# Opening the pool of layer 1's modulation weights ahead of layer 0's down-phase pools, and issuing its first loads there

## The chip, the cores and the metric

The kernel runs on one core of one Trainium2 chip. The metric is the device time of one execution in microseconds (us), the median of several runs. The core has five engines that each execute their own instructions in order: TensorE (PE, with weight loads listed as PEld), VectorE (DVE), ScalarE (ACT), GpSimd (POOL) and SyncE (SP). Nearly all transfers are issued by SP, in its order, as DMAs.

## The reference, cut to what matters

Two layers work on 512 latent and 256 context tokens of width 1024. Each has a mixing part and a feed-forward part, and six modulation vectors come from a product of the conditioning vectors with `ada_w`, 1024 by 6144 per layer.

```python
for l in range(DEPTH):
    mod_l = (jax.nn.silu(c) @ ada_w[l] + ada_b[l])[:, None, :]
    mod_c = (jax.nn.silu(c_ctx) @ ada_w[l] + ada_b[l])[None, None, :]
    sh1, sc1, gt1, sh2, sc2, gt2 = jnp.split(mod_l, 6, axis=-1)
    ...
    p_l = modulate(rms_norm(lat, norm_mix_pre[l]), sh1, sc1) @ w_in[l]
    ...
    mixed_l = jnp.concatenate([gla_l, ssd_l, ret_l], axis=-1) @ w_out[l]
    lat = lat + gt1 * rms_norm(mixed_l, norm_mix_post[l])
    h_l = modulate(rms_norm(lat, norm_ffn_pre[l]), sh2, sc2)
    lat = lat + gt2 * rms_norm(swiglu(h_l, ffn_w13[l], ffn_w2[l]), norm_ffn_post[l])
```

## The kernel before, in words

All tokens stay on one core, as six blocks of 128. Float32 products are made from two rounded parts, a high and a low one (`whi` and `wlo` of weights, `hidhi` and `hidlo` of the hidden activations, two `H` tiles of the normed input), in three matmuls each. A scheduler orders the instructions of each engine by a time model and the priorities of the program's order; the order that it chose is what the engines execute.

Modulation. Layer 0's vectors 0 and 1 are made at the start. The others are made in "steps" by the class `Ada`: a step takes one block of 128 by 1024 weights, `araw` (512 KB), loaded at L195, and multiplies it with the conditioning vectors in four small matmuls (L203 and L206), eight steps to a vector, into the accumulator `pa`. `pa` comes from a pool of one buffer (L93), `araw` from three (`NRAW`, L248). `ada.some(n)` puts n steps at a place of the program; inside, up to three loads are issued ahead of the first step. After eight steps `ada_finish` (L208) takes the accumulator out: for the two gate vectors it clears a tile on GpSimd, loads the bias into it in four pieces (L216), adds the sums on VectorE (L217) and stores the row in four pieces (L219); for the others ScalarE copies it (L221). Layer 0 makes its own vectors 2 to 5 and layer 1's 0 and 1 (48 steps), layer 1 its own 2 to 5 (32 steps), first the gate 2.

Pools. `adp` of a layer (opened at L595) holds a table of constants, `cst2` (843 KB), and the `araw` tiles; once the mixing part is over, `cst2` and two `araw` buffers hold parts of the feed-forward's input, `b11h` and `b11l` (L1197, L1198), for the up phase. It is closed at L1419, and the pools of the down phase are opened where it lay (`D0` at L1420). Layer 1's `adp` is opened at the head of layer 1, in the place that the down phase's pools have left; a new tile waits for the tiles that it overlaps.

Down phase of layer 0. Two passes of 512 columns read the hidden activations back from DRAM (`hr`, two loads of 768 KB at a time) and multiply them (L1407). The second pass ends in the back part, `ffn_back`, block by block: post-norm, addition to the residual rows `x` (L337), a store to `xsd` (L338), and layer 1's first norm: ScalarE's `xn`, eight transposes (L306), modulation (L312 and L314), and the split into `H` (L317 and L318). The rows `x` are loaded from `xsd` (L322) into two buffers. Layer 1 begins with the projection `gv` (L644; L498 into `mm`), 24 matmuls for each of the six blocks, and with `small` (72 matmuls), whose results ScalarE copies out at L681.

Of the kernel before, what the change touches and what calls it, by code (L numbers as in the profile page):

```python
# [77 lines left out]
CST, COFF, MSK = _constants()  # L78
NC0 = COFF["ident"][1]
# [3 lines left out]
def tile_backbone(ctx: ExitStack, tc: tile.TileContext, a: dict, out: bass.AP, dbg=None):  # L83
    nc = tc.nc
    V, S, G, PE, DMA = nc.vector, nc.scalar, nc.gpsimd, nc.tensor, nc.sync
# [15 lines left out]
    def pt(pool, tag, shape, dt=F32, bufs=None):  # L101
        kw = {} if bufs is None else {"bufs": bufs}
        return pool.tile(shape, dt, tag=tag, name=tag, **kw)

    def pool(name, bufs=1, side="left"):
        return tc.tile_pool(name=name, bufs=bufs, side=side, reuse_waits="tile")
# [4 lines left out]
    cst = [pt(pp, "cst", [128, NC0])]  # L111
# [6 lines left out]
    def C(k, shape=None, **ax):  # L118
        o, n = COFF[k]
        v = cst[0][:, o:o + n] if o < NC0 else cst[1][:, o - NC0:o - NC0 + n]  # L120
        return v.rearrange(shape, **ax) if shape else v
# [6 lines left out]
    def hpair():  # L128
        t = [pt(hp, "H", [128, 8, T], F32R) for _ in range(2)]
        return t, [h.bitcast(F32) for h in t]  # L130
# [60 lines left out]
    def ada_load(ap, l, kind, part, nparts, k0, bufs):  # L191
        w = 1024 // nparts
        c0 = 1024 * kind + w * part
        raw = pt(ap, "araw", [128, nparts, w], bufs=bufs)
        DMA.dma_start(raw, kblk(a["ada_w"][l, 128 * k0:128 * (k0 + nparts), c0:c0 + w]))  # L195
        return raw

    def ada_step(ps, raw, kb, g_w):
        first = None
        for g in range(4):  # L200
            args = ps[32 * g:32 * g + 32, :g_w], sil[:, kb, :], raw[:, g_w * g:g_w * g + g_w]
            if first is None:
                first = PE.matmul(*args, start=kb == 0, stop=kb == 7)  # L203
            else:
                with tc.high_priority(offset=2000), tc.issue_after(first.ins):
                    PE.matmul(*args, start=kb == 0, stop=kb == 7)  # L206
# [41 lines left out]
    NRAW = 3  # L248

    class Ada:  # L250
        def __init__(self, ap, tasks):
            self.ap = ap
            self.todo = [(l, kind, kb) for l, kind in tasks for kb in range(8)]
            self.raws = []

        def some(self, n):
            for _ in range(min(n, len(self.todo))):
                while len(self.raws) < min(NRAW, len(self.todo)):
                    l, kind, kb = self.todo[len(self.raws)]
                    self.raws.append(ada_load(self.ap, l, kind, 0, 1, kb, NRAW))  # L260
                l, kind, kb = self.todo.pop(0)
                if kb == 0:
                    self.ps = psa.tile([128, 512], F32, tag="pa", name="pa")
                ada_step(self.ps, self.raws.pop(0)[:, 0], kb, 256)
                if kb == 7:
                    ada_finish(self.ap, l, kind, 0, 1, self.ps, NRAW)

    def kblk(src):
        return src.rearrange("(k p) n -> p k n", p=128)
# [50 lines left out]
    def x_tile(np_, xin, bufs=2):  # L320
        x = pt(np_, "x", [128, D], bufs=bufs)
        DMA.dma_start(x, xin)  # L322
        return x
# [17 lines left out]
    def load_gw(gp, np_, l, w, rs_):  # L341
        gw = pt(gp, "gw", [128, 2, D], bufs=1)
        wpt = pt(np_, "xn", [128, D])
        src = a["norm_mix_post"] if w == 0 else a["norm_ffn_post"]
        DMA.dma_start(wpt, src[l:l + 1, :].to_broadcast([128, D]))
        for r in rs_:
            DMA.dma_start(gw[:, r], gts[l, w, r:r + 1, :].to_broadcast([128, D]))
            G.tensor_tensor(gw[:, r], gw[:, r], wpt, ALU.mult)
        return gw
# [233 lines left out]
    G.tensor_copy(msk, mskf)  # L583
    st_.close()

    for l in range(NL):
        last = l == NL - 1
        u = U[l]
# [2 lines left out]
        segs_out = [LAT] if last else [LAT, CTX]  # L591
        tbs_all = [4, 5, 0, 1, 2, 3]
        tbs_out = [0, 1, 2, 3] if last else tbs_all
        ax = ctx.enter_context(ExitStack())
        adp = ax.enter_context(pool(f"adp{l}", 2))  # L595
        cst[1:] = [pt(adp, "cst2", [128, CST.shape[1] - NC0], bufs=1)]
        S.dma_start(cst[1], a["cst"][:, NC0:])
        ones = C("ones")
        tri = C("tri", "p (a f) -> p a f", a=2)
        gam = C("gam", "p (h f) -> p h f", h=4)  # L600
# [46 lines left out]
        with ExitStack() as sx:  # L647
# [134 lines left out]
            with pool(f"Sb{l}") as Sb, tc.high_priority(offset=300):  # L782
# [23 lines left out]
                def ssd_out(tb, Sf, Sbw):  # L806
# [47 lines left out]
                                            bc(eG[:, tb, 8 * d:8 * d + 8], 64), ALU.mult)  # L854
                            (V if d else G).tensor_tensor(y, y, y1, ALU.add)
                    DMA.dma_start(yds[l][tsl, :], y)

                ada = Ada(adp, [(l, kind) for kind in range(2, 6)] + ([] if last else [(l + 1, 0), (l + 1, 1)]))

                sf = sb = None  # L860
                for tbs in ([4, 5], [0, 1, 2, 3]):
# [410 lines left out]
        def hid_load(hr, f, q=None):  # L1272
            return DMA.dma_start(hr, hview[:, f:f + 2])

        def hid_split(hr, hi, lo):
            for q in range(2):
                S.copy(hi[:, q], hr[:, q])  # L1277
                (G if q else V).tensor_tensor(lo[:, q], hr[:, q], hi[:, q].bitcast(F32), ALU.subtract)  # L1278
            return hi, lo
# [137 lines left out]

        fx.close()
        ax.close()  # L1419
        with pool(f"D{l}") as Dp:  # L1420
            y0 = pt(Dp, "y0", [128, npos, 512], bufs=1)

            order = [f for pi in range(2) for f in range(0 if pi else 4, NF, 2)]
            fetched = []

            def hid_fetch():
                if order:
                    hr = pt(Dp, "hr", [128, 2, tot], bufs=2)
                    ins = hid_load(hr, order[0])
                    fetched.append((order.pop(0), hr))  # L1430
                    return ins.ins

            def hid_pair(f):
                g, hr = fetched.pop(0)
                assert g == f
                pair = hid_split(hr, *(pt(Dp, t, [128, 2, tot], F32R, bufs=3) for t in ("hidhi", "hidlo")))
                hid_fetch()
                return pair

            with tc.high_priority(offset=60):  # L1440
                hid_fetch()
                fetch2 = hid_fetch()

            dx = ctx.enter_context(ExitStack())
            back = {}

            def begin_back():
                nf = dx.enter_context(pool(f"nf{l}", 2))
                gw = load_gw(Dp, nf, l, 1, [0] if last else [0, 1])
                if last:  # L1450
                    xs = [x_tile(nf, xsd[128 * tb:128 * tb + 128, :], 4) for tb in tbs_out]
                else:
                    H["t"], H["f"] = hpair()

                def ffn_back(pos, ps):
                    tb = tbs_out[pos]
                    tsl = slice(128 * tb, 128 * tb + 128)
                    dst = out[0, tsl, :] if last else xsd[tsl, :]
                    cut = last and pos == npos - 1
                    x = xs[pos] if last else x_tile(nf, xsd[tsl, :])  # L1460
                    x = post_norm(nf, [y0[:, pos], ps], x, gw[:, 0 if tb < 4 else 1], dst, cut)
                    if not last:
                        pre_norm(nf, l + 1, 0, tb, x)

                return ffn_back

            for pi, (j, poss) in enumerate(u["passes"]):
                pss = first if pi == 0 else acc_tiles(pi)
                if pi == 1:
                    back = begin_back()  # L1470
                f = 0
                for gi, gn in enumerate(GROUPS):
                    if pi or gi > 1:
                        with nullcontext() if pi or gi > 2 else tc.issue_after(fetch2):
                            un = get(u["w2"][gi, pi])
                    ks = [k0 for k0 in range(0, gn, 2) if pi or f + k0 >= 4]
                    if gi + 1 < len(GROUPS):
                        for k0 in ks:
                            hh = hid_pair(f + k0)
                            for pos, ps in zip(poss, pss):  # L1480
                                down(ps, hh, un, k0, pos, f + k0)
                    else:
                        hs = [hid_pair(f + k0) for k0 in ks]
                        prev = None
                        for pos, ps in zip(poss, pss):
                            for k0, hh in zip(ks, hs):
                                down(ps, hh, un, k0, pos, f + k0)
                            if j == 0:
                                (S.copy if pos % 2 else V.tensor_copy)(y0[:, pos], ps)
                                continue  # L1490
                            if prev is not None:
                                back(*prev)
                            prev = pos, ps
                        if prev is not None:
                            back(*prev)
                    f += gn
            dx.close()
# [20 lines left out]
```

## Time and profile before

| | |
|---|---|
| median of 3 runs | 1870.13 us (1869.07 to 1879.29) |
| the profiled execution, its own time | 1874.65 us |
| its span, first to last instruction | 1872.9 us |
| mean granted TensorE clock, share of full | 0.962 |
| PE busy | 1740.0 us (93%) |
| DVE busy | 1170.5 us (62%) |
| ACT busy | 793.2 us (42%) |
| POOL busy | 571.0 us (30%) |

The times in all views are counted from the span's start. A row of the view of stretches gives the stretch, its length, then the busy time of PE, PEld, DVE, ACT and POOL with the number of instructions in brackets, and last the granted clock as a share of full speed, the busy share of the 16 DMA engines and GB/s. A row of the timeline gives start, duration, engine, line, operation, output<-input, shape and the number of merged instructions; in brackets stands the idle time before it and what ended it. "SPq" is the issue of a DMA, not its transfer. Matmul durations overlap, so two successive starts tell the pace. A grouped row gives a line's instructions with their number, busy time, mean duration in ns, and then the engine's idle time before them with its causes. A row of the DMA view gives the transfers issued, their number and the size of each.

### The profile page before, as it was taken

What the parts mean: (1) busy time and instruction counts of PE and PEld (TensorE: products, weight loads), DVE (VectorE), ACT (ScalarE), POOL (GpSimd) and SP (SyncE); (2) the same over time, 40 slices, a digit from 0 to 9 for tenths busy, and PEclk for the clock granted to TensorE, in tenths of its full rate; (3) what the DMA queues carried; (4) which work ended last, traced back from release to release, by engine and by line L of the source; (5) the groups of instructions that cost most, each with busy time, mean ns of one, the idle gap of its engine ahead of it and who ended that gap; (6) DMA issues with size and microseconds to landing.
All of it is one profiled execution on the core that took longest, in us unless ns stands there. A gap on an engine that the chain in (4) does not pass through costs nothing. (4 is left out here: it accounts for less than half of the span.)

```text
span 1872.9 us, 30314 instructions
## 1 busy us (share of the span) xinstructions
PE 1740.0 (93%) x11851; PEld 1571.3 (84%) x11851; DVE 1170.5 (62%) x1981; ACT 793.2 (42%) x1433; POOL 571.0 (30%) x569
## 2 busy tenths in 40 slices
PE   5999899998879999999999989999987979999998
PEld 3778887798868999999888767898876969999886
DVE  4586777467557755555433436678856567888455
ACT  3545343225654333333333466444424544444343
POOL 1002622114403433222422240073303126555322
PEclk9999998999989999999999989999977979999999
DMA  8435476514324433332746373355613245444753
GB/s 288 175 103 172 130 214 216 185 46 163 128 68 132 135 94 113 104 94 64 270 138 200 112 230 130 113 159 160 228 47 119 89 125 161 125 132 130 249 203 133
DMA packets 239228, 275.15 MB, mean 147 GB/s; under 512 B 14056, under 2 KB 182476, under 8 KB 239084
## 3 DMA queue, kind: packets, MB, share of 16 engines
q1 hardware_dynamic: 237872, 271.30, 45.2%
q8 instruction: 93, 1.52, 0.3%
q10 hardware_dynamic: 1212, 1.91, 0.3%
q14 instruction: 51, 0.42, 0.1%
HBM read 234.24 MB, written 38.93 MB: 146 GB/s over the span
## 5 line engine op out<-in xcount | busy, mean ns | idle before, releaser
L369 DVE TENSOR_TENSOR wlo<-raw,whi 128x1024 fp32r<-128x1024 f32 (+2 forms) x192 | 266.6, 1395 | 154.0 <-ACT whi L368 153.7
L1324 PE MATMUL px<-H,whi 128*128 128x384 f32 (+1 forms) x1408 | 307.4, 310 | 9.7 <-ACT whi L368 9.5
L368 ACT CAST whi<-raw 128x1024 fp32r<-128x1024 f32 (+2 forms) x192 | 193.9, 1018 | 221.0 <-PE px L1324 86.0
L498 PE MATMUL mm<-whi,H 128*128 128x256 f32 x1376 | 273.9, 294 | 9.7 <-ACT stg L630 4.6
L1324 PEld LDWEIGHTS px<-H,whi 128*128 128x128 f32 x1408 | 235.2, 190 | 12.2 <-ACT whi L368 11.5
L498 PEld LDWEIGHTS mm<-whi,H 128*128 128x128 f32 x1376 | 223.6, 196 | 23.8 <-issue 11.3
L1324 PE MATMUL px<-H,wlo 128*128 128x384 f32 (+1 forms) x704 | 211.1, 310 | 0.0
L498 PE MATMUL mm<-wlo,H 128*128 128x256 f32 x688 | 200.7, 292 | 0.0
L498 PE MATMUL mm<-H,whi 128*128 128x256 f32 (+2 forms) x640 | 160.8, 341 | 6.3 <-ACT xp L759 4.2
L368 ACT CAST whi<-S 128x1024 fp32r<-128x1024 f32 x88 | 73.5, 835 | 165.0 <-DVE S L419 85.0
L498 PEld LDWEIGHTS mm<-wlo,H 128*128 128x128 f32 x688 | 135.4, 197 | 3.7 <-issue 2.9
L1324 PEld LDWEIGHTS px<-H,wlo 128*128 128x128 f32 x704 | 131.3, 190 | 0.7 <-DVE wlo L369 0.6
L498 PEld LDWEIGHTS mm<-H,whi 128*128 128x128 f32 (+1 forms) x640 | 109.4, 190 | 25.5 <-ACT xp L759 6.0
L498 PE MATMUL px<-whi,H 128*128 128x256 f32 x640 | 121.2, 289 | 9.6 <-DVE H L1236 4.4
L1278 POOL TENSOR_TENSOR hidlo<-hr,hidhi 128x768 fp32r<-128x768 f32 (+1 forms) x40 | 70.8, 1771 | 178.0 <-ACT hidhi L1277 167.1
L1359 POOL TENSOR_TENSOR hf<-hf,g 128x384 f32<-128x384 f32 (+1 forms) x44 | 55.8, 1269 | 224.4 <-issue 147.0
L369 DVE TENSOR_TENSOR wlo<-S,whi 128x1024 fp32r<-128x1024 f32 x88 | 89.3, 1015 | 40.6 <-ACT whi L368 40.5
L498 PEld LDWEIGHTS px<-whi,H 128*128 128x128 f32 x640 | 101.2, 193 | 13.7 <-ACT H L1235 6.3
L498 PE MATMUL mm<-H,wlo 128*128 128x256 f32 (+3 forms) x320 | 108.5, 339 | 0.0
L1407 PE MATMUL px<-wlo,hidhi 128*128 128x512 f32 x276 | 107.5, 389 | 0.0
L1407 PE MATMUL px<-whi,hidhi 128*128 128x512 f32 x276 | 106.4, 389 | 0.0
L1407 PE MATMUL px<-whi,hidlo 128*128 128x512 f32 x276 | 105.7, 389 | 0.0
(334 smaller groups left out, 4089.4 us busy)
## 6 DMA issues: line engine op xcount, KB each, us to landing
raw<-ffn_w_dram SPq DMA_DIRECT2D x100, 512.0 KB
araw<-ada_w_dram SPq DMA_DIRECT2D x96, 512.0 KB
raw<-w_in_dram SPq DMA_DIRECT2D x26, 1024.0 KB
raw<-ffn_w_dram SPq DMA_DIRECT2D x20, 1024.0 KB
hr<-hd SPq DMA_DIRECT2D x22, 768.0 KB
hr<-hd SPq DMA_DIRECT2D x22, 512.0 KB
Rt<-gd SPq DMA_DIRECT2D x40, 256.0 KB
hd<-hf SPq DMA_DIRECT2D x22, 384.0 KB
```

Of the source, the lines that this page charges most:

```text
L368: S.copy(hi, src)
L369: lo_engine.tensor_tensor(lo, src, hi.bitcast(F32), ALU.subtract)
L498: PE.matmul(ps, x(k), y(k), start=(k == 0 and p == 0), stop=(k == total - 1 and p == 2))
L1278: (G if q else V).tensor_tensor(lo[:, q], hr[:, q], hi[:, q].bitcast(F32), ALU.subtract)
L1324: PE.matmul(ps[:, :hn], w[x][:, k], r[y](k), start=first and k == 0 and p == 0, stop=k == 3 and p == 2, skip_group_check=True)
L1359: G.tensor_tensor(h1, h1, g1, ALU.mult)
L1407: PE.matmul(ps, lh[x](k), rh[y](k), start=f + k == 0 and p == 0, stop=f + k == NF - 1 and p == 2, skip_group_check=True)
```

## The change

Layer 1's `adp` is opened before the pools of layer 0's down phase, right where layer 0's is closed, and so lies in its place beside them; its table of constants is loaded there. The `Ada` of a layer is made with the pool. A new method `fetch` issues the loads that the buffers have room for, and is called for layer 1's at the second pass of layer 0's down phase. The calls of `some` stay where they were.

```diff
+        def fetch(self):
+            while len(self.raws) < min(NRAW, len(self.todo)):
+                l, kind, kb = self.todo[len(self.raws)]
+                self.raws.append(ada_load(self.ap, l, kind, 0, 1, kb, NRAW))
+
         def some(self, n):
             for _ in range(min(n, len(self.todo))):
-                while len(self.raws) < min(NRAW, len(self.todo)):
-                    l, kind, kb = self.todo[len(self.raws)]
-                    self.raws.append(ada_load(self.ap, l, kind, 0, 1, kb, NRAW))
+                self.fetch()
...
+    def open_ada(l):
+        ax = ctx.enter_context(ExitStack())
+        adp = ax.enter_context(pool(f"adp{l}", 2))
+        cst[1:] = [pt(adp, "cst2", [128, CST.shape[1] - NC0], bufs=1)]
+        S.dma_start(cst[1], a["cst"][:, NC0:])
+        return ax, adp
...
-        ax = ctx.enter_context(ExitStack())
-        adp = ax.enter_context(pool(f"adp{l}", 2))
-        cst[1:] = [pt(adp, "cst2", [128, CST.shape[1] - NC0], bufs=1)]
-        S.dma_start(cst[1], a["cst"][:, NC0:])
+        if l == 0:
+            ax, adp = open_ada(0)
+            ada = Ada(adp, [(l, kind) for kind in range(2, 6)] + [(l + 1, 0), (l + 1, 1)])
...
-                ada = Ada(adp, [(l, kind) for kind in range(2, 6)] + ([] if last else [(l + 1, 0), (l + 1, 1)]))
...
         fx.close()
         ax.close()
+        if not last:
+            ax, adp = open_ada(l + 1)
+            ada = Ada(adp, [(l + 1, kind) for kind in range(2, 6)])
         with pool(f"D{l}") as Dp:
...
                 if pi == 1:
                     back = begin_back()
+                    if not last:
+                        ada.fetch()
```

The scheduler moves more than the three loads. On SP, in the back part, the kernel before has these rows (`x_10173` and `x_10219` are the residual rows of the fifth and sixth block, `araw_12143` the weights of layer 1's first step):

```order
L338 DMA xsd_89<-x_10057 128x1024
L322 DMA x_10173<-xsd_89 128x1024
L338 DMA xsd_89<-x_10115 128x1024
L322 DMA x_10219<-xsd_89 128x1024
L640 DMA vd1_93<-stg_10317 128x256
L338 DMA xsd_89<-x_10173 128x1024
L640 DMA vd1_93<-stg_10345 128x256
L195 DMA araw_12143<-ada_w_dram 128x1024
L195 DMA araw_12145<-ada_w_dram 128x1024
L195 DMA araw_12147<-ada_w_dram 128x1024
```

The same place of the changed kernel (`x_10184` and `x_10230` are the fifth and sixth block; `araw_12172`, `12178`, `12380` and `12386` the weights of steps 7 to 10, `araw_12392` the bias row after step 8, `araw_12403` step 11):

```order
L195 DMA araw_12172<-ada_w_dram 128x1024
L195 DMA araw_12178<-ada_w_dram 128x1024
L195 DMA araw_12380<-ada_w_dram 128x1024
L341 DMA xsd_89<-x_10126 128x1024
L325 DMA x_10184<-xsd_89 128x1024
L195 DMA araw_12386<-ada_w_dram 128x1024
L216 DMA araw_12392<-ada_b_dram 2x256 x3
L325 DMA x_10230<-xsd_89 128x1024
L216 DMA araw_12392<-ada_b_dram 2x256
L341 DMA xsd_89<-x_10184 128x1024
L219 DMA gts_88<-araw_12392 2x256 x4
L195 DMA araw_12403<-ada_w_dram 128x1024
```

Before, the loads of the steps stood behind all `x` loads; now loads 4 to 6 stand ahead of these rows, 7 to 10 between them, and from load 11 on they follow the gate's stores. The first three loads stand at the end of the up phase, around its last but one `hd` store.

On TensorE, the kernel before has its first step here, after the first block of the latents is begun (`mm_10348` is the third block's projection):

```order
L498 MATMUL mm_10348<-whi_9897,H_9448 128x256
L306 MATMUL px_10195<-cst_75,xn_10193 128x128 x4
L306 MATMUL px_10207<-cst_75,xn_10193 128x128 x4
L498 MATMUL mm_10348<-whi_9901,H_9447 128x256
L498 MATMUL mm_10348<-wlo_9902,H_9447 128x256
L203 MATMUL pa_12149<-araw_12143,sil_104 32x256
L206 MATMUL pa_12149<-araw_12143,sil_104 32x256 x3
L498 MATMUL mm_10348<-whi_9901,H_9448 128x256
```

In the changed kernel this is the place of step 17, the first into the accumulator `pa_12559`, with what stands ahead of it and behind it (`xn_10250` is the sixth block; the rows for steps 13 to 15 stand between the transposes and the first row):

```order
L203 MATMUL pa_12405<-araw_12434,sil_104 32x256
L206 MATMUL pa_12405<-araw_12434,sil_104 32x256 x3
L203 MATMUL pa_12559<-araw_12538,sil_104 32x256
L206 MATMUL pa_12559<-araw_12538,sil_104 32x256 x3
L501 MATMUL mm_10354<-whi_9908,H_9452 128x256
L501 MATMUL mm_10354<-wlo_9909,H_9452 128x256
L501 MATMUL mm_10354<-whi_9908,H_9453 128x256
```

Steps 1 to 3 now stand right behind the last matmul of the down phase, and all of steps 1 to 17 stand ahead of the projections of the last four blocks (`mm_10354` is the first of them) and of `small`; before, eight steps stood in this stretch, the first of them inside the third block's projection.

## Rows read from the trace of the kernel before

**Rows 1.** Stretches: length, PE, PEld, DVE, ACT, POOL, clock, DMA, GB/s.

```profile
877.00:887.00 10.00, 10.00 (x60) 10.00 (x59) 3.50 (x7) 2.64 (x5) 1.01 (x1) 1.00 0.11 41
905.00:922.00 17.00, 17.00 (x76) 14.04 (x76) 7.62 (x5) 5.38 (x7) 9.96 (x5) 1.00 0.93 343
1070.25:1124.75 54.50, 43.35 (x327) 36.80 (x327) 22.58 (x45) 33.99 (x74) 22.54 (x28) 0.87 0.71 226
1091.00:1103.00 12.00, 6.42 (x38) 5.17 (x37) 3.74 (x8) 6.02 (x12) 4.61 (x4) 0.72 0.91 308
1125.00:1250.00 125.00, 122.29 (x805) 104.34 (x804) 85.88 (x129) 63.37 (x105) 27.25 (x33) 0.99 0.41 130
1370.00:1430.00 60.00, 42.34 (x246) 35.14 (x246) 36.36 (x92) 19.32 (x43) 6.08 (x13) 0.66 0.21 68
```

**Rows 2.** Timeline of TensorE, 1069 to 1119 (a step is two such records).

```profile
1069.88 0.39 PE L1407 MATMUL px<-whi,hidlo 128*128 128x512 f32 x1
...
1097.77 0.64 PE L203 MATMUL pa<-araw,sil 128*32 128x256 f32 x1 [5.22 <-DMA araw<-ada_w_dram]
...
1099.59 0.63 PE L498 MATMUL mm<-whi,H 128*128 128x256 f32 x2
...
1100.22 0.63 PE L498 MATMUL mm<-whi,H 128*128 128x256 f32 x2
...
1105.42 0.40 PE L498 MATMUL mm<-whi,H 128*128 128x256 f32 x2
...
1105.78 0.40 PE L498 MATMUL mm<-whi,H 128*128 128x256 f32 x2
...
1117.89 0.40 PE L203 MATMUL pa<-araw,sil 128*32 128x256 f32 x1
...
1118.35 0.38 PE L203 MATMUL pa<-araw,sil 128*32 128x256 f32 x1
```

**Rows 3.** Timeline of ScalarE: two casts that waited, and the last `small` copy.

```profile
919.80 1.57 ACT L1277 CAST hidhi<-hr 128x768 fp32r<-128x768 f32 x2 [3.94 <-DMA hr<-hd]
...
927.97 1.57 ACT L1277 CAST hidhi<-hr 128x768 fp32r<-128x768 f32 x2 [2.44 <-DMA hr<-hd]
...
1124.75 0.57 ACT L681 COPY lr<-mm 32x512 f32<-32x512 f32 x1 [5.31 <-PE mm L498]
```

**Rows 4.** Groups of TensorE's instructions from 1070.25 to 1124.75.

```profile
L498 PE MATMUL mm<-whi,H 128*128 128x256 f32 x96 | 22.8, 326 | 2.1 <-POOL H L318 1.7 <-ACT H L317 0.5
...
L306 PE MATMUL px<-cst,xn 128*128 128x128 f32 x44 | 7.6, 321 | 3.8 <-DVE y L331 2.1 <-ACT hh L312 1.4 <-ACT xn L297 0.3
...
L203 PE MATMUL pa<-araw,sil 128*32 128x256 f32 x16 | 5.2, 420 | 5.2 <-DMA araw<-ada_w_dram 5.2
```

**Rows 5.** Timeline of SP's issues, 1080 to 1093.

```profile
1080.27 0.32 SPq L322 DMA_DIRECT2D x<-xsd  x1
...
1086.18 0.32 SPq L322 DMA_DIRECT2D x<-xsd  x1
...
1090.94 2.61 SPq L195 DMA_DIRECT2D araw<-ada_w_dram  x3
```

**Rows 6.** Timeline of VectorE: the fifth block's addition to the residual rows.

```profile
1085.24 1.21 DVE L337 TENSOR_TENSOR x<-x,y 128x1024 f32<-128x1024 f32 x1
```

**Rows 7.** Timeline of SP's issues in the down phase's first pass.

```profile
907.79 2.27 SPq L1273 DMA_DIRECT2D hr<-hd  x2
...
923.38 2.88 SPq L1273 DMA_DIRECT2D hr<-hd  x2
```

**Rows 8.** DMA issues from 1070 to 1130, with the size of each.

```profile
araw<-ada_w_dram SPq DMA_DIRECT2D x11, 512.0 KB
raw<-w_in_dram SPq DMA_DIRECT2D x2, 1024.0 KB
xsd<-x SPq DMA_DIRECT2D x4, 512.0 KB
x<-xsd SPq DMA_DIRECT2D x3, 512.0 KB
```

## The prediction

> **What bounds the kernel now.** I began with the busy time by stage. After layer 0's feed-forward TensorE is the bound nearly everywhere: from 1125 to 1250 it is busy 122.29 of 125 us, and only from 1370 to 1430 does it wait for others for long (42.34 of 60) [rows 1]. In between lies the stretch the change is about: from the end of the down phase (the last matmul starts at 1069.88 [rows 2]) to ScalarE's copy of the last `small` product at 1124.75 [rows 3]. There TensorE is busy 43.35 of 54.50 us, so 11.15 us are idle [rows 1]. The grouped view says who ends that idle time: 5.2 us the first load of layer 1's modulation weights, 3.8 us the transposes of the back part, some 2 us the split activations [rows 4]. The timeline shows the 5.2 us as one wait, and behind it a slow patch: three projection matmuls (a pair and its third) take 0.63 us there (1099.59 to 1100.22) and 0.36 us later (1105.42 to 1105.78) [rows 2], with a mean granted clock of 0.72 from 1091 to 1103 [rows 1], a mixture of 1.2 and 2.4 GHz. The wait exists because SP issues those loads only at 1090.94 [rows 5] and the first step starts at 1097.77 [rows 2].
>
> The same stretch has a second clock, the back part's six blocks. Each needs its residual rows `x` loaded into one of two buffers, and the load can go only when the store of an earlier block has landed. The fifth block's load goes at 1080.27 [rows 5], and VectorE adds it at 1085.24 without having waited [rows 6]: the loads arrive just in time, with nothing to spare.
>
> The last view is the queue. SP issues two `hr` loads from 907.79 on [rows 7] behind a batch of other loads, and ScalarE gets the first at 919.80, 12 us later [rows 3]; one `hr` load issued at 923.38 with nothing ahead [rows 7] is used at 927.97 [rows 3], 4.6 us. Transfers on SP's queue are served in turn. From 905 to 922 they moved 343 GB/s with the 16 engines 93% busy, from 1091 to 1103 308 GB/s at 91% [rows 1]. I take 343; the lone load (0.79 MB, 2.3 us at that rate) then has 2.3 us besides its bytes.
>
> The Trainium skill says the same of the queue in "DMA: Bandwidth & Descriptors", section "Queues, rings and completion order": each of the engines takes a ring's descriptors in order. It speaks against this change, since whatever is put on SP ahead of an `x` load delays it; the 12 us row agrees.
>
> **The change, part by part.** *Three loads and the constants, early.* They now wait for the last reading of `b11l` and `b11h`, at the end of the up phase. DMA there is 11% busy (877 to 887 [rows 1]), TensorE is full and asks for none of them, so I cost them at 0; without that gap they would cost 1.57 MB and 0.86 MB at 343 GB/s, 7 us of transfers. Layer 0's steps do not move at all: 0.
>
> *Steps 1 to 3 behind the last down matmul.* A step takes 0.46 us (1117.89 to 1118.35 [rows 2]), so 1.4 us, which fit into the idle 2.1 us before the transposes that wait for VectorE [rows 4]: 0. So far the change does what it says: the first step no longer waits.
>
> *What is late next.* With the first steps done early the scheduler has placed 17 steps, not 8, ahead of the last 96 projection matmuls (four blocks of 24) and the 72 of `small`. But only three buffers exist, so loads 4 to 17 are issued from about 1071 on, each when an earlier step frees a buffer. They share SP with the back part: while a load there waits for its step, the block's `xsd` store and the next `x` load stand behind it, and VectorE's add waits for that. From the sizes [rows 8], before step 17 can run the queue has to move 14 weight loads (7.34 MB), three `x` loads (1.57), four `xsd` stores (2.10) and one `w_in` unit (1.05): 12.06 MB, at 343 GB/s 35.2 us. From 1070.8 plus 2.3 that is 1108.3: the earliest end for the loads.
>
> Following the order of SP, it is later. The third `xsd` store is behind 3.67 MB counting itself: landed at 1070.8 + 2.3 + 10.7 = 1083.8. Only then can the fifth `x` load go (1080.27 before), behind loads 7 to 9 and a store: 6.29 MB in all, landed at 1091.4, 6 us after VectorE's add of before (1085.24). The bias row of the gate follows; its four loads queue behind load 10 and the sixth `x`: 7.34 MB, 1094.5. VectorE adds it only after the fifth block's add, and the accumulator `pa` is a single buffer, so step 9 waits for that too. Then come four small stores, and SP reaches load 11 at about 1097. Loads 11 to 17 and one store are 4.19 MB: 1097 + 2.3 + 12.2 = 1111.5, step 17 done at 1112.
>
> TensorE executes in order, so the 96 matmuls stand behind it: 32 threes at 0.36 us = 11.5; a slow start as behind the wait of before, six threes at 0.64 instead of 0.36, 1.7; `small`, 24 threes, 8.6. End: 1133.8 against 1124.75: +9.1 us. What comes back: nine steps (17 less 8) no longer stand in the stretch after 1125, where TensorE is the bound: 9 x 0.46 = 4.1. **Sum: +5.0 us.** Against the profiled execution's 1874.65 that is 1879.7; that execution lies 4.5 above the median of the runs, so for the median 1875.
>
> Bounds: loads never held back by anything but bytes give 1108.3 and +1.8; 308 GB/s instead of 343 adds 4 us, and if the nine steps give nothing back it is +13. I stay near the middle because the 343 is measured with a full queue, as this one will be. Other costs, not in the trace of before: tiles of the down phase now lie where the up phase's tiles lay. Between nothing and the landing of the last `hf` store, which `hr` now has to wait for; that store is issued well before `hr` is wanted, so 0, at worst the 2.3 us that a transfer has besides its bytes. Later parts of layer 1 are reordered slightly on all engines; with TensorE 122.29 of 125 busy, there are 2.7 us to win or lose.
>
> By the fit of the Trainium skill, "DMA: Bandwidth & Descriptors", section "Anatomy of one DMA" (2 us and 436 GB/s), the 12.06 MB would be moved in 29.7 us instead of 37.5 and the sum would fall by 7.8 us to -2.8; an estimate, and the row with 343 GB/s at 93% speaks against it.
>
> **Rivals.** *A, faster.* The loads keep up after all: because stores and loads overlap better than a served-in-turn queue, the steps find their weights as steps 2 to 8 do now (only one of 16 step records waits [rows 4]). Then the 5.2 us wait goes and nine steps fall into idle time: -5.2 - 4.1 = -9.3, median 1860.8. Against it: 17 steps in the 40 us until 1110 with 12 MB are 300 GB/s sustained, while the stretch moves 226 now [rows 1]. It decides if `x` of the fifth block still arrives by about 1086.
>
> *B, clearly slower.* The delay of `small` is not paid back: from its copy starts the chain of gates and scans on ScalarE and VectorE which TensorE's in-order stream meets later, and with nine steps fewer between, TensorE arrives there too early. VectorE is busy 85.88 of 125 us from 1125 to 1250 [rows 1], so the chain cannot run much faster. +9.1 to +13: 1879 to 1883, about 1881. It decides when TensorE idles over 4.1 us more than now between 1125 and 1250.
>
> *C, nothing in the end.* The stretch from 1370 to 1430, where TensorE idles 17.7 us [rows 1], hangs on a chain of its own that takes up a delay or a gain: 1870, within 3.
>
> **How the numbers follow.** About 0.5% (9.4 us) is what a measurement of this kernel can tell from no change. Forecast 0.42, A 0.26, B 0.26, C 0.06. The forecast's own range is 1869 to 1883 (its bounds, and the 2.7 us of reordering below), of which a tenth or so (0.05) lies over the bound of slower. A lies on its own bound: 0.15 faster, 0.11 the same. B is 0.25 slower by its upper end and what else may be lost, 0.01 the same. So faster 0.15, same 0.55, slower 0.30. The range reaches from A's time to past B's: 1860 to 1886.
>
> **What would show it.** Right: no wait for a load at step 1; the constants and three weight loads issued at about 878; the fifth block's `x` add at 1090 or later; TensorE waiting for `araw` loads or for `pa` between 1090 and 1112, more than 5.2 us in sum; the copy of `small` at 1130 to 1136; DMA over 85% busy from 1075 to 1110. Wrong: the `x` add still near 1085, the copy of `small` at or before 1124, or a wait at the start of the down phase that is new. The prediction fails upward if the scans after `small` then stall TensorE, downward if the queue moves the 12 MB in less than 30 us.

## The result

The changed kernel takes 1887.4 us (median of six runs, 1885.2 to 1892.1) against 1870.4 for the kernel before on the same chip: a ratio of 1.008, 95% interval 1.0061 to 1.0099, so 11 to 18 us slower. The forecast was 1875 and its range ended at 1886. The profiled execution took 1892.11 us (span 1890.3).

On the page of the changed kernel TensorE's share stays at 93%; its busy time grew by 16.5 us although no matmul was added.

```profile
span 1890.3 us, 30302 instructions
PE 1756.5 (93%) x11851; PEld 1578.6 (84%) x11851; DVE 1161.8 (61%) x1981; ACT 793.2 (42%) x1433; POOL 565.4 (30%) x569
```

The two traces were laid side by side, each instruction against its like. They differ by 3.1 us in the changed kernel's favour before the change has done anything (another execution). Then it loses in three places.

**The down phase, where no loss was expected.** The first fence is the kernel before, grouped by shape from 950 to 1060, the second the changed kernel (line, operation, tiles, count, busy us, mean ns, idle).

```profile
L1407 PE MATMUL px<-whi,hidlo 128*128 128x512 f32 x113 | 44.0, 389 | 0.0
```
```profile
L1414 PE MATMUL px<-whi,hidlo 128*128 128x512 f32 x108 | 42.8, 397 | 0.0
```

Each down matmul's record is 8 ns longer, and in the same 110 us five fewer of this kind are started. Two starts lie 235 ns apart (999.88 to 1002.70 for twelve) instead of 227. TensorE is busy without a gap, its granted clock is 1.00 in both (1000 to 1025), and no DMA or cast is waited for. From the first matmul that reads `hidhi` (906.42 before, 903.36 changed) to the last down matmul (1069.88 and 1072.23) the lag grows by 5.4 us.

**The transition.** Stretches of the changed kernel (columns as in [rows 1]): the end of the up phase, the transition up to the copy of `small`, the part of it that the prediction named, and the slow patch.

```profile
877.00:887.00 10.00, 10.00 (x59) 10.00 (x59) 3.31 (x6) 1.63 (x3) 1.01 (x1) 1.00 0.77 257
1072.60:1140.40 67.80, 51.53 (x413) 39.44 (x413) 23.97 (x47) 36.59 (x76) 22.25 (x28) 0.82 0.64 222
1075.00:1110.00 35.00, 23.08 (x170) 14.70 (x169) 17.84 (x40) 25.84 (x55) 19.28 (x24) 0.76 0.85 306
1088.80:1109.60 20.80, 13.10 (x84) 7.78 (x84) 8.93 (x20) 13.00 (x27) 11.51 (x17) 0.60 0.74 264
```

The three loads and the constants are where they were expected: DMA busy 77% at the end of the up phase instead of 11% [rows 1]. From the end of the last down matmul to the copy of `small` 67.8 us pass instead of 54.5, with 16.3 idle instead of 11.2. TensorE's timeline (1072 to 1118; in brackets the idle time and what ended it):

```profile
1072.23 0.40 PE L1414 MATMUL px<-whi,hidlo 128*128 128x512 f32 x1
1072.56 0.40 PE L203 MATMUL pa<-araw,sil 128*32 128x256 f32 x1
...
1088.24 0.40 PE L203 MATMUL pa<-araw,sil 128*32 128x256 f32 x1 [2.10 <-DMA araw<-ada_w_dram]
...
1097.40 0.64 PE L203 MATMUL pa<-araw,sil 128*32 128x256 f32 x1 [3.81 <-DVE araw L217]
...
1106.28 0.63 PE L203 MATMUL pa<-araw,sil 128*32 128x256 f32 x1 [2.92 <-DMA araw<-ada_w_dram]
...
1117.43 0.58 PE L501 MATMUL mm<-whi,H 128*128 128x256 f32 x1
```

Step 1 no longer waits. Among steps 4 to 17 TensorE waits eight times for weights (11.4 us in all) and once for `pa`, and the third block's projection starts at 1117.43, 45.2 us behind the last down matmul and behind all of these steps. So far this is the predicted picture. ScalarE's timeline holds a row that was not in it:

```profile
1115.99 0.37 ACT L221 COPY araw<-pa 128x256 f32<-128x256 f32 x1 [3.70 <-DMA araw<-ada_w_dram]
1116.26 0.66 ACT L639 COPY stg<-mm 128x256 f32<-128x256 f32 x2
...
1140.38 0.58 ACT L690 COPY lr<-mm 32x512 f32<-32x512 f32 x1
```

ScalarE copies the first projection's result out of `mm` only at 1116.26, 44.0 us behind the last down matmul. In the kernel before it does so 14.7 us behind it:

```profile
1084.57 0.36 ACT L630 COPY stg<-mm 128x256 f32<-128x256 f32 x1
```

`mm` has two buffers. As long as the first two projections stand in them, a third can't begin, whatever TensorE waits for meanwhile. The reason is where the tiles lie (bytes within a partition, from the built programs):

```
tile                     before              changed
hidhi, first buffer      135200 to 141344    154240 to 160384
hh, two buffers          205152 to 209248    224192 to 228288
stg, three buffers       224672 to 227744    224672 to 227744
```

The down phase's pools now start 19,040 bytes higher. Their last tile, `hh` of the back part, reaches into `stg`, which layer 1's pool holds at the upper end of memory. A `stg` copy has to wait until the back part has read for the last time the buffer of `hh` that it overlaps, on GpSimd:

```profile
1111.29 2.50 POOL L321 TENSOR_TENSOR H<-hh,H 128x512 fp32r<-128x512 f32 x2 [2.52 <-ACT H L320]
```

GpSimd is done at 1113.8. The last 2.5 us until 1116.26 are not the block's: in ScalarE's order the copies stand behind the one at L221, shown above, which waits 3.70 us for a step's weights.

**After the transition.** Some of it comes back, then more is lost. ScalarE's copy of `gqk`, before and changed:

```profile
1214.47 0.59 ACT L880 COPY gqk<-mm 128x512 f32<-128x512 f32 x1 [4.06 <-PE mm L498]
```
```profile
1225.60 0.59 ACT L887 COPY gqk<-mm 128x512 f32<-128x512 f32 x1 [4.10 <-PE mm L501]
```

At `small` the changed kernel was 15.6 us late (1140.38 against 1124.75 [rows 3]), here it is 11.1: 4.5 came back. At the end of the spans it is 17.4: 6.3 more are lost.

### The profile page after: what moved, and what is told of

Read it like the earlier page. It is cut to its first block, busy times and chain, and to the rows that moved or that the text cites. A ratio compares the mean times of both kernels' runs of the same rounds, so it can differ in the third digit from the quotient of the medians.

```text
span 1890.3 us, 30302 instructions
## 1 busy us (share of the span) xinstructions
PE 1756.5 (93%) x11851; PEld 1578.6 (84%) x11851; DVE 1161.8 (61%) x1981; ACT 793.2 (42%) x1433; POOL 565.4 (30%) x569
## 5 line engine op out<-in xcount | busy, mean ns | idle before, releaser
L372 DVE TENSOR_TENSOR wlo<-raw,whi 128x1024 fp32r<-128x1024 f32 (+2 forms) x192 | 265.5, 1390 | 168.5 <-ACT whi L371 168.2
```

What stands on the lines that cost most here:

```text
L372: lo_engine.tensor_tensor(lo, src, hi.bitcast(F32), ALU.subtract)
```

## Experiments

In the table all lags are in us from the start of the last down matmul of the same profile; "pace" is the mean record of a down matmul (ns); the ratio is to the kernel before, run on the same chip in the same rounds.

```
kernel                            pace  fifth x add  first stg  small  ratio (95%)
before                            389   15.4         14.7       54.9   1
changed                           397   22.0         44.0       68.2   1.0080 (1.0061-1.0099)
changed, run again                397   21.1         40.3       65.1   1.0093 (1.0065-1.0122)
changed, 32 bytes                 395   20.9         42.4       67.9   1.0110 (1.0081-1.0138)
before, 32 bytes                  396   15.3         14.7       54.6   1.0028 (1.0013-1.0043)
changed, steps held               397   17.7         37.9       62.9   1.0043 (1.0019-1.0067)
both of these                     395   17.0         37.9       61.8   1.0045 (1.0027-1.0062)
changed, stg low                  397   22.2         28.4       55.6   1.0025 (1.0006-1.0044)
before, back part high            389   15.3         36.3       63.8   1.0044 (1.0023-1.0065)
stg low, 416 bytes                389   22.7         28.9       57.4   1.0011 (0.9992-1.0030)
pool early, no early call         397   20.8         40.2       65.3   1.0117 (1.0084-1.0150)
stg low, 416 bytes, steps held    389   17.0         24.8       53.7   0.9974 (0.9957-0.9990)
stg low, 416 bytes, loads held    389   15.4         21.9       56.3   0.9995 (0.9978-1.0013)
```

**First: place or company, steps or opening.** At this point the theory for the transition was still the prediction's. A tile that nothing uses moves the down phase's pool by 32 bytes, in the changed kernel and in the kernel before:

```diff
         with pool(f"D{l}") as Dp:
+            if not last:
+                pt(Dp, "skew", [128, 8], bufs=1)
             y0 = pt(Dp, "y0", [128, npos, 512], bufs=1)
```

> The changed kernel with an unused tile of 32 bytes per partition as the first tile of layer 0's down-phase pool, which moves that pool's tiles (y0, hr, hidhi, hidlo) by 32 bytes; nothing else. Theory P (place): the down matmuls are slower by where their stationary tiles begin (a multiple of 64 bytes in the changed kernel, 32 beyond one before); then they pace at 227 ns again instead of 234, the down phase gives back the 5 us that it lost, and the median is about 1882, ratio to before 1.006. Rival Q (company): they are slower because of the transfers and reads of the other engines beside them; then 234 ns stays, and 1887.

> The kernel before with the same unused tile of 32 bytes in layer 0's down-phase pool. Theory P: the down matmuls pace at 234 ns instead of 227, about 730 of them, so +5 us: about 1875.5, ratio 1.003. Rival Q: 227 ns and 1870, ratio 1.000.

The kernel before becomes slower by nothing but 32 bytes: 396 ns, its last down matmul 4.7 us later against the first that reads `hidhi`, ratio 1.0028. The order on every engine is unchanged, so Q falls. But P named the wrong remainder: the changed kernel, moved to 32 beyond a multiple of 64, runs at 395 and not at 389.

```profile
L1407 PE MATMUL px<-whi,hidlo 128*128 128x512 f32 x108 | 42.7, 396 | 0.0
```

The steps from the fourth on are held behind the last projection `gv`:

```diff
-                ada_step(self.ps, self.raws.pop(0)[:, 0], kb, 256)
+                self.n += 1
+                with tc.issue_after(self.gate) if self.gate is not None and self.n > 3 else nullcontext():
+                    ada_step(self.ps, self.raws.pop(0)[:, 0], kb, 256)
...
+            ada.gate = proj_b("gv", tbs_all, to_dram(vds[l], 0))
```

> The changed kernel, with layer 1's steps from the fourth on queued on TensorE behind the last projection gv; so three steps, not 17, stand ahead of the last 96 projection matmuls, and only loads 4 to 6 share SP with the back part. Theory S (steps ahead): the loss up to the copy of small is theirs; the fifth block's x add comes within 15 us of the last down matmul again (15.4 before, 21.9 in the changed kernel), small is copied 47 to 52 us behind it (54.5 before, 67.8 changed), and with the slower down phase still in it the median is 1866 to 1874. Rival T: the loss comes from opening the pool and the new order of layer 1 behind 1250; then small is early but the time stays above 1878.

> Both edits: the steps from the fourth on behind the last gv, and the tile of 32 bytes. By P and S the two gains add: 5 us below the run with the steps held alone, 1861 to 1869, ratio to before 0.995 to 0.999, the lowest of these kernels. By Q and T no better than that run.

Both missed, by 10 and 14 us (medians 1883.9 and 1883.4, before 1873.9). With only three steps ahead, `small` is still copied 62 to 63 us behind the down phase. TensorE's timeline of the run with the steps held says why:

```profile
1107.89 1.97 PE L312 MATMUL px<-cst,xn 128*128 128x128 f32 x8 [4.06 <-ACT xn L303]
1116.96 0.58 PE L504 MATMUL mm<-whi,H 128*128 128x256 f32 x1 [7.10 <-ACT stg L644]
```

The third block's projection waits 7.10 us for the `stg` copy and starts 38.3 us behind the last down matmul, in both of these kernels. So the steps and their loads explain only the smaller part of the delay: in the changed kernel that projection starts at 45.2, in its second run (below) at 41.9. Most of the steps filled a time in which the projections couldn't run. Theory S fell as stated, and T too, since `small` was not early.

**Second: the blocked copies.** The buffers of `stg` for `gv` are taken from a pool of their own, at the place of the down phase's `hr`:

```diff
-        def to_dram(dr, c0, mode=None):
+        def to_dram(dr, c0, mode=None, sp=Ms):
             def evac(tb, ps):
-                sg = pt(Ms, "stg", [128, 256], bufs=3)
+                sg = pt(sp, "stg", [128, 256], bufs=3)
...
-            proj_b("gv", tbs_all, to_dram(vds[l], 0))
+            with pool(f"gv{l}") as Gv:
+                pt(Gv, "skip", [128, 3072], bufs=1)
+                proj_b("gv", tbs_all, to_dram(vds[l], 0, sp=Gv))
```

> The changed kernel, with the three stg buffers into which ScalarE copies the projection gv of layer 1 taken from a pool of their own at the place of layer 0's hr tiles, instead of the pool at the upper end of memory, where in the changed kernel the back part's hh tiles overlap them. Theory B (blocked copies): in the changed kernel no stg copy can run before the back part's last reading of hh, mm has two buffers, so the projections of blocks 3 to 6 and small wait for the end of the back part; freed, the third block's projection starts within 18 us of the last down matmul (45 us in the changed kernel), small is copied within 57 us of it (67.8 changed, 54.5 before), and what stays is mainly the slower down phase: median ratio to before 0.997 to 1.004. Theory S (queue and steps, the prediction's): the weight loads on SP ahead of the x loads do it; the fifth x add stays 21 us behind, small over 62 us, ratio 1.006 or more.

And the reverse, the kernel before with the back part's tiles where the changed kernel has them:

```diff
                 gw = load_gw(Dp, nf, l, 1, [0] if last else [0, 1])
+                if not last:
+                    pt(nf, "skip", [128, 4760], bufs=1)
```

> The kernel before, with an unused tile of 19040 bytes in the pool of the back part ahead of its x, y and hh tiles: these lie where they lie in the changed kernel, hh over the stg buffers; y0, hr, hidhi and hidlo stay, and so do the loads of layer 1's weights behind the x loads. Theory B: the projections of blocks 3 to 6 wait for the end of the back part here too, small is copied 60 us or more behind the last down matmul (54.5 before), with the down phase at its 227 ns: ratio 1.003 to 1.007. Theory S: nothing is early on SP, so no change: 54 to 55 us, ratio 0.998 to 1.002.

Both came out as theory B says, but for one figure. Freed, the `small` copy comes 12.5 us earlier, with the fifth `x` add as late as in the changed kernel; the scheduler now puts the third block's projection ahead of steps 11 and later by itself. That projection starts 29.2 us behind the last down matmul, not within 18: ScalarE's order has the two copies behind its work on the fifth block, whose `x` row is late.

```profile
1101.24 0.56 PE L501 MATMUL mm<-whi,H 128*128 128x256 f32 x1
```
```profile
1100.47 0.64 ACT L639 COPY stg<-mm 128x256 f32<-128x256 f32 x2
...
1127.72 0.58 ACT L692 COPY lr<-mm 32x512 f32<-32x512 f32 x1
```

Blocked, the kernel before loses 8.9 us at `small` and 0.4% in all, with its first three loads, its `x` rows and its down phase as they were. ScalarE's timeline of that kernel shows the copies right behind the last split of the back part, the second of them released by GpSimd's reading of `hh`:

```profile
1102.04 0.62 ACT L317 CAST H<-hh 128x512 fp32r<-128x512 f32 x1
1102.56 0.37 ACT L630 COPY stg<-mm 128x256 f32<-128x256 f32 x1
1104.03 0.37 ACT L630 COPY stg<-mm 128x256 f32<-128x256 f32 x1 [1.10 <-POOL H L318]
...
1130.09 0.58 ACT L681 COPY lr<-mm 32x512 f32<-32x512 f32 x1
```

Two more kernels: the freed one with a tile of 416 bytes on top (`[128, 104]` in the first diff), and the change without its `ada.fetch()`:

> As the run with the low stg buffers, and an unused tile of 416 bytes at the head of layer 0's down-phase pool, so that its tiles begin at the same remainder of 512 bytes as in the kernel before (32; 128 in the changed kernel, 64 and 160 in the two runs with 32 bytes). Theory R (remainder of 512): the down matmuls pace at 227 ns and the down phase costs nothing more than before, 5 us less than the run without it: ratio 0.992 to 1.000. Rival: the pace hangs on the place in some other way; 231 to 234 ns stay, and the ratio is that of the run without the tile.

> The change without its call that issues the first loads at the second pass: only the pool's place and the early table of constants. TensorE's order is that of the changed kernel, since the scheduler finds the three buffers free and puts the loads early by itself. Theories B and R: all of the loss comes with the pool's place, ratio 1.006 to 1.011 as for the changed kernel. Rival: the call itself costs or saves something; ratio outside of that.

With the remainder of 512 bytes restored the pace is that of the kernel before to the nanosecond:

```profile
L1416 PE MATMUL px<-whi,hidhi 128*128 128x512 f32 x112 | 43.6, 389 | 0.0
```

The ratio, 1.0011, is a little above the range expected for it; the interval holds 1. Without the call the kernel is as slow as with it (65.3 us to `small`, ratio 1.0117, above the expected 1.011 but with an interval that overlaps the changed kernel's). The reason is plain: the built program is the changed kernel's, with the same instructions in the same order at the same addresses on every engine, the first three loads at the end of the up phase included. So opening the pool is enough for all of the change, and this is one more run of the changed kernel. It does not tell the place from the early loads; the kernel before with the back part high (no early loads) and the freed one with 416 bytes (early loads, both faults of the place mended) do.

**Third: what was left.** With both faults mended the fifth `x` add was still 22.7 us behind and `small` at 57.4. Two ways of taking weight loads off its path: hold the steps from the fourth on behind the third block's projection (as above, with `proj_b` returning the last matmul of every block, and `[2]` of these as the gate), or hold the loads on SP behind the last `x` load:

```diff
-                self.raws.append(ada_load(self.ap, l, kind, 0, 1, kb, NRAW))
+                self.m += 1
+                with tc.issue_after(self.lgate) if self.lgate is not None and self.m > 3 else nullcontext():
+                    self.raws.append(ada_load(self.ap, l, kind, 0, 1, kb, NRAW))
...
+            if not last:
+                ada.lgate = xlast[0]
```

> As the run with the low stg buffers and the tile of 416 bytes, and the steps from the fourth on queued on TensorE behind the third block's projection gv (the first block of the latents). Only loads 4 to 6 then stand ahead of the back part's x loads on SP. What stayed in that run: the fifth x add 22.4 us behind the last down matmul (15.0 before), small copied at 57.4 (54.5 before). Theory S-rest: that lag is the weight loads ahead of the x loads, so the add comes at 16 to 18 us, small at 49 to 53, and the ratio is 0.993 to 0.999. Rival: the lag comes from elsewhere (TensorE's order, the clock); the small copy stays over 55 us and the ratio at 1.000 or more.

> The same base, and instead of the steps the loads from the fourth on are queued on SP behind the sixth block's x load, so that nothing but the first three loads of layer 1 is ahead of the x loads. S-rest: the fifth x add comes at 15 us as before, small is copied at 49 to 54, ratio 0.993 to 0.999. Rival: the steps then wait for their weights in the projections (as in the kernel before, 5.2 us) and small stays at 54 us or later; ratio 0.998 to 1.002.

> The changed kernel itself once more, beside the others on the same chip. If the sum of the two causes (5 us in the down phase, 13 us up to small of which 4 to 5 come back) is all of the loss, its ratio is 1.006 to 1.010 again; if 1.011 and more, as two kernels with its order had (1.011 and 1.0117), a part of the loss that changes from chip to chip stands behind the transition too, in the stretches from 1350 to 1450 with their low clock.

The changed kernel itself, run again beside them, came to 1.0093, in the first of its two ranges. Holding the steps gives the one kernel that beats both: 0.9974, with an interval below 1. Its `x` add and ratio are as S-rest said, `small` at 53.7 a little later than the 53 given as the limit. Holding the loads brings the `x` add back to its old place, but then `small` comes at 56.3 and the ratio is 0.9995, as the rival said. In the profile of that kernel, from its last down matmul to `small`, the steps wait for their weights again:

```profile
L203 PE MATMUL pa<-araw,sil 128*32 128x256 f32 x26 | 8.8, 444 | 4.7 <-DMA araw<-ada_w_dram 4.6
```

In the kernel with the steps held no step waits in that stretch:

```profile
L203 PE MATMUL pa<-araw,sil 128*32 128x256 f32 x16 | 4.4, 386 | 0.0
```

## Why the prediction was right or wrong, step by step

**What bounds the kernel** was read rightly: the 5.2 us wait, the `x` rows with nothing to spare, SP's queue in turn.

**Three loads and constants early, steps 1 to 3 free:** right as far as the profile shows. TensorE is busy for all of the 10 us with DMA at 77%, and step 1 does not wait.

**The queue:** right, and near in size. SP's timeline of the changed kernel has the fifth block's `x` load at 1086.13, and VectorE adds it at 1094.18:

```profile
1086.13 0.33 SPq L325 DMA_DIRECT2D x<-xsd  x1
```
```profile
1094.18 1.22 DVE L340 TENSOR_TENSOR x<-x,y 128x1024 f32<-128x1024 f32 x1
```

Counted from the last down matmul that is 6.6 us later than before [rows 6]; 6 were forecast. The wait for `pa` came too (3.81 us). Step 17 was done some 45 us behind the last down matmul where 42 were forecast: from 1075 to 1110 the queue moved 306 GB/s at 85% busy, not 343, and the estimate with 436 GB/s was further off still.

**"96 projection and 72 small matmuls behind it":** in TensorE's order this is what happened. The third block's projection starts right behind step 17, and from there to the copy of `small` 22.95 us pass where 21.8 were forecast. The sum gave +9.1 at `small`, the profile +13.3; 3 of the 4 us are step 17's. What the prediction did not see is why the order is so: with the `stg` copies blocked that projection did not start before 38.3 us even with three steps. The other steps ahead of it and their loads added 3.6 to 6.9 us to that. With the copies free the scheduler itself puts 10 steps ahead of it instead of 17, and steps and queue then cost `small` 0.7 to 2.5 us (55.6 and 57.4 against 54.9). No run has 17 steps ahead and the copies free, so what the forecast order would cost by itself is not shown.

**"Pool placement 0, at worst 2.3":** this is the step that failed. It asked only which earlier tiles the down phase's tiles now cover, and priced one wait for a store. It missed which later tiles are covered at the upper end (`stg`; shown alone by the run of the kernel before with the back part high, 8.9 us at `small`, ratio 1.0044), and that a matmul's pace can hang on the place of its tiles (shown alone by the kernel before moved by 32 bytes, about 5 us, ratio 1.0028). The two alone add to 0.7%, nearly the whole loss of 0.8 to 0.9%; with both mended in the changed kernel the ratio is 1.0011.

**Nine steps paid back, -4.1:** the size came, 4.5 by the copy of `gqk`, but by luck. Between the copy of `small` and that of `gqk` only two steps are gone, 0.9 us (a step is two of these records; before from 1124.75 to 1214.5, changed from 1140.38 to 1225.6):

```profile
L498 PE MATMUL mm<-H,whi 128*128 128x512 f32 (+1 forms) x274 | 70.3, 347 | 2.6 <-ACT xp L759 2.6
...
L203 PE MATMUL pa<-araw,sil 128*32 128x256 f32 x18 | 5.2, 388 | 0.0
```
```profile
L501 PE MATMUL mm<-H,whi 128*128 128x512 f32 (+1 forms) x265 | 67.5, 344 | 1.1 <-ACT xp L768 1.1
...
L203 PE MATMUL pa<-araw,sil 128*32 128x256 f32 x14 | 4.0, 388 | 0.0
```

The rest is fewer other matmuls in the stretch and 1.5 us less wait for `xp`. The kernel with 416 bytes and the steps held has nine steps there, as before, and the stretch still takes 86.1 us, against 89.7 before and 85.2 changed. The other seven steps could come back only behind `gqk`, where the changed kernel loses.

**The new sum:** down phase +5.4, transition +13.3, paid back -4.5: +14.2, against a measured +11 to +18. Behind `gqk` the profiled execution loses 6.3 more, which with the 3.1 us it was ahead at the start makes the 17.4 between the two spans. The median lies 1.4 us above the upper end of the range; by the ratio, on the forecast's 1870.1, it is 1885 and just inside. Either way the range holds no term for what happened: it reaches 1886 as a margin past rival B, while the forecast's own range ended at 1883 and its sum said +5.0.

**The signs.** The early loads, the late `x` add and TensorE's waits for weights and `pa` from 1090 to 1112 (8.7 us) came as named. The copy of `small` at 1140.38 is later than the 1130 to 1136 given for it. The slower pace of the down phase and the blocked copies stood in none of them.

**The rivals.** A (the loads keep up) and C (absorbed later) did not happen. B, not paid back, is the nearest in size (1883 at most, 1887.4 measured) but not in mechanism: 4.5 us came back. The bound that B gave, TensorE idle more than now from 1125 to 1250, did not occur (123.41 busy of 125, against 122.29 [rows 1]).

**What stays open.** The 6.3 us lost behind `gqk`. In the list of waits from 1230 to 1480, TensorE waits 5.3 us in two pieces for a `stg` that VectorE writes, where the kernel before waits 3.0 in one; and its clock from 1390 to 1450 is 0.56, where the kernel before has 0.66 from 1370 to 1430 [rows 1]:

```profile
PE mm L501 <- DVE stg L637: 5.3, 2, 2.9
```
```profile
1390.00:1450.00 60.00, 44.31 (x208) 37.12 (x209) 31.82 (x80) 16.49 (x36) 5.95 (x11) 0.56 0.18 56
```

The three other profiles with the changed kernel's order lost 5.9 (run again), 5.1 (no early call) and 14.4 us (32 bytes) there, the kernel before with the back part high 5.3. The kernel before moved by 32 bytes, with the old order on all engines, loses 3.9, so part of such a difference is what one execution has against another. The six kernels with the copies free or the steps held lie between 3.3 us gained and 1.4 lost. No run separates order from clock, and the ratios of the single causes above include what each lost here.

## What to carry to other kernels

When a pool is opened ahead of another, write down the addresses of all tiles before and after, and for each tile that now covers another ask who writes it next: a wait for memory can be longer than the wait that the move was meant to remove, and it stands in no row of the old trace. A scheduler that fills a gap with movable work makes that work look like the cause; look at who holds the accumulators (here two `mm` buffers) before blaming what runs in the gap. The Trainium skill, "Perfetto Trace Analysis", section "Matmuls", states that independent groups of matmuls should rotate through different accumulator banks, so that the evacuation of one overlaps the matmuls of the next. Here two buffers rotated, and in the run with the steps held TensorE still waited 7.10 us, because the evacuation itself had no place to write.

## What the runs showed of the hardware

The 128x512 matmuls of the down phase have records 1.5 to 2% longer, and starts further apart (233 to 235 ns over twelve instead of 227), by where the pool's tiles lie. The pool's start, as a remainder of 512 bytes, and the mean record: 32: 389 ns (before, before with the back part high, and the three kernels with 416 bytes), 64: 396, 128: 396 to 397 (five kernels), 160: 395 (two). The granted clock from 1000 to 1025 was 1.00 in every one of these kernels, and the weight tiles `whi` and `wlo`, which are the moving operand here, began at a remainder of 32 throughout. Whether it is the remainder itself, or that both operands have the same, was not tried, nor which of the pool's tiles counts. The Trainium skill, "SBUF — State Buffer", section "Operand start alignment", states where an operand may start and says that this is about legality, not speed; all of these starts are legal by it, and the runs show that they differ in speed.
